# Gate and up of 15 of 22 FFN chunks by seven block products for eight, with the token sums held where x and f were

## The chip, the cores and the metric

The kernel runs on one core of a Trainium2 chip. The metric is the device time of one execution in microseconds (us). The engines are TensorE (PE, matmuls; PEld its weight loads), VectorE (DVE), ScalarE (ACT), GpSimd (POOL) and SyncE (SP, which issues most of the DMAs). Each works through its own queue in order; semaphores tie them together.

## The reference

Two layers of a backbone with 640 tokens (128 context, 512 latent) and 1024 features. Each layer is a half-step FFN, a token mixer and a second half-step FFN, each between norms with gains, shifts and gates that come from a conditioning vector (the modulation). The part that matters here is the FFN:

```python
D_MODEL, D_FF, DEPTH = 1024, 2816, 2        # 128 context and 512 latent tokens

def swiglu(h, w_gu, w_dn):
    g, u = jnp.split(h @ w_gu, 2, axis=-1)
    return (jax.nn.silu(g) * u) @ w_dn

    # in a layer, three times with other weights (the middle one is the mixer):
    mods = (silu(cond) @ w_mod[l] + b_mod[l]).reshape(Bc, 9, 1, D_MODEL)
    f = swiglu(pre(x, 0), w_ffn_gu[l, 0], w_ffn_dn[l, 0])
    x = x + 0.5 * mods[:, 2] * rmsnorm(f, g_post[l, 0])
```

## The kernel before, in words

Features lie on the partitions, tokens along the free axis. Every fp32 operand is kept as a pair (h, lo) with h + lo the value, and every product is three matmuls: h h, lo h, h lo. A matmul takes 128x128 weights and 320 tokens, half of the 640. The input of an FFN is `self.h`, two tiles [128, 8, 640]; the residual x and the branch f are two more tiles of that size, and the four share the slots A to D.

D_FF is 22 chunks of 128. A gate or an up of a chunk (`gate`, `up`) is 8 feature chunks x 3 x 2 halves = 48 matmuls. ScalarE takes the tanh of the gate, DVE makes gate times sigmoid (L535) and the product with up (L540), and the result is split again (L165 ScalarE, L166 DVE) into `act`. `PARTS` cuts the chunks in 7, 7, 8; after each of the first two parts eight `down` tasks (one for 128 features of the output) multiply `act` with the down weights and put or add the result into f on DVE.

The middle of an FFN works on both halves of the tokens. Its two ends are by halves: `boundary` runs the tail of one stage (for an FFN: two chunks and the eight last downs) for one half of the tokens and then the other, and the norm chains (`chain`) of the finished half beside the other half's products; the first five chunks of the next FFN (`NHEAD`) follow in the same way. `STEPS` says how many steps of a chain go ahead of each task.

What comes when on an engine is the order in which `run` emits the tasks. Each weight unit (128 x 1024 for gate and up) is loaded by SP into a ring of three `raw` tiles and split by `split` (ScalarE: wh, DVE: wl, rings of three); `advance` emits the splits two units ahead of the task that uses them. `self.later` holds the splits of activations back until those are out. `self.side` is a generator of modulation steps for later layers (`mods`): one step loads 512 KB of w_mod (two `wm` buffers) and runs two 1024-wide reductions on DVE (L294). Tasks of the middle emit one each (`side`), and whatever is left is emitted by `end` when the FFN is over. The first FFN has 48 such steps to do, the second 48, the third 32, the fourth none.

PSUM tiles are [128, 2, 512], four of them. GpSimd (L334, L340, L446, L917) and the DMAs on its queue work for the norm chains and the mixers.

## Time and profile before

| what | value |
|---|---|
| median of 3 runs | 3243.14 us (3242.57 to 3244.58) |
| span of the profiled execution | 3243.3 us, 50877 instructions |
| PE busy | 3117.2 us, 20988 matmuls |
| DVE busy | 2005.3 us |
| ACT busy | 1162.5 us |
| POOL busy | 496.5 us |
| DMA | 381.51 MB, mean 118 GB/s |

Busy times are of one engine; they overlap. The span is from the first to the last instruction of the execution that was profiled, and the single runs above were made without the profiler. A stretch (a window of the span) gives the busy time of each engine in it, the granted clock of TensorE as a share of full speed (PEclk; full is 2.4 GHz) and the mean busy share of the 16 DMA engines. Line numbers are those of the kernel before; helpers such as `split` and `projs` carry the lines of very many instructions.

### The profile page before, as it was taken

What the parts mean: (1) busy time and instruction counts of PE and PEld (TensorE: products, weight loads), DVE (VectorE), ACT (ScalarE), POOL (GpSimd) and SP (SyncE); (2) the same over time, 40 slices, a digit from 0 to 9 for tenths busy, and PEclk for the clock granted to TensorE, in tenths of its full rate; (3) what the DMA queues carried; (4) which work ended last, traced back from release to release, by engine and by line L of the source; (5) the groups of instructions that cost most, each with busy time, mean ns of one, the idle gap of its engine ahead of it and who ended that gap; (6) DMA issues with size and microseconds to landing.
All of it is one profiled execution on the core that took longest, in us unless ns stands there. A gap on an engine that the chain in (4) does not pass through costs nothing.

```text
span 3243.3 us, 50877 instructions
## 1 busy us (share of the span) xinstructions
PE 3117.2 (96%) x20988; PEld 3081.5 (95%) x20988; DVE 2005.3 (62%) x2880; ACT 1162.5 (36%) x1919; POOL 496.5 (15%) x413
## 2 busy tenths in 40 slices
PE   7999998899999989999989999989999999899997
PEld 6999998899999979999989999989999998899997
DVE  7667649876653485676785663678665436723346
ACT  4222235454432452212452212463444325422123
POOL 4000015500011330000230000244000113200004
PEclk9999999999999999999999999999999999999999
DMA  5454433311122334454434442442111323322223
GB/s 190 170 171 153 145 112 133 128 64 63 58 97 86 133 130 157 149 174 151 137 128 158 150 148 74 134 159 75 66 52 64 103 94 132 129 80 69 82 92 117
DMA packets 118718, 381.51 MB, mean 118 GB/s; under 512 B 13651, under 2 KB 30867, under 8 KB 117461
## 3 DMA queue, kind: packets, MB, share of 16 engines
q1 hardware_dynamic: 115348, 359.73, 33.3%
q0 software_dynamic: 2848, 18.35, 1.5%
q8 instruction: 165, 2.70, 0.3%
q14 instruction: 69, 0.56, 0.1%
q10 hardware_dynamic: 288, 0.17, 0.0%
HBM read 363.88 MB, written 14.32 MB: 117 GB/s over the span
## 4 chain that ended last, share of the span: by engine, by line
PE 80%; DVE 13%; issue 3%; ACT 3%; POOL 0%; DMA 0%; SPq 0%; DVEq 0%; ACTq 0%; POOLq 0%
PE ps L230 74%; DVE wl L166 3%; PE ps L211 2%; PE ps L213 2%; PE ps L212 2%; DVE slotD L366 1%; ACT wh L165 1%; DVE W L1039 1%; DVE slotB L366 1%; DVE t L402 1%; PE ps L257 1%; PE ps L1030 1%; DVE junk L1285 1%; DVE s L340 1%; DVE t L246 0%
## 5 line engine op out<-in xcount | busy, mean ns | idle before, releaser
L166 DVE TENSOR_TENSOR wl<-raw,wh 128x1024 fp32r<-128x1024 f32 (+1 forms) x493 | 616.1, 1251 | 258.3 <-ACT wh L165 247.8
L165 ACT CAST wh<-raw 128x1024 fp32r<-128x1024 f32 (+1 forms) x493 | 507.4, 1032 | 661.9 <-issue 407.2
L230 PE MATMUL ps<-slotA,wh 128*128 128x320 f32 x2272 | 584.6, 313 | 6.1 <-ACT wh L165 3.8
L230 PE MATMUL ps<-slotA,wl 128*128 128x320 f32 x2272 | 580.6, 312 | 6.3 <-DVE wl L166 6.2
L230 PE MATMUL ps<-slotD,wh 128*128 128x320 f32 x2272 | 570.0, 313 | 17.0 <-DVE slotD L1317 15.0
L230 PE MATMUL ps<-slotB,wh 128*128 128x320 f32 x2272 | 580.2, 311 | 3.1 <-DVE slotB L423 1.6
L230 PE MATMUL ps<-act,wh 128*128 128x320 f32 x2816 | 568.5, 310 | 7.6 <-DVE act L166 4.0
L230 PE MATMUL ps<-slotC,wh 128*128 128x320 f32 x2272 | 570.5, 313 | 3.8 <-ACT slotC L413 1.9
L230 PEld LDWEIGHTS ps<-act,wh 128*128 128x128 f32 x2816 | 455.3, 189 | 10.1 <-DVE act L166 5.2
L230 PEld LDWEIGHTS ps<-slotD,wh 128*128 128x128 f32 x2272 | 396.8, 190 | 19.9 <-DVE slotD L1317 16.2
L230 PEld LDWEIGHTS ps<-slotA,wl 128*128 128x128 f32 x2272 | 399.0, 190 | 10.3 <-DVE wl L166 9.2
L230 PEld LDWEIGHTS ps<-slotA,wh 128*128 128x128 f32 x2272 | 398.6, 190 | 9.3 <-ACT wh L165 4.8
L230 PEld LDWEIGHTS ps<-slotB,wh 128*128 128x128 f32 x2272 | 398.5, 190 | 4.5 <-DVE slotB L423 2.2
L230 PEld LDWEIGHTS ps<-slotC,wh 128*128 128x128 f32 x2272 | 396.7, 191 | 5.4 <-ACT slotC L413 2.1
L446 POOL TENSOR_TENSOR s<-s,t 128x320 f32<-128x320 f32 x84 | 118.3, 1408 | 1693.4 <-ACT t L445 1693.2
L230 PE MATMUL ps<-act,wl 128*128 128x320 f32 x1408 | 363.1, 309 | 0.0
L230 PE MATMUL ps<-slotC,wl 128*128 128x320 f32 x1440 | 348.3, 312 | 1.3 <-DVE wl L166 1.1
L294 DVE CUSTOM_DVE_ANT_0 junk<-wm,sc,par 128x1024 bf16<-128x1024 f32 x256 | 328.2, 1282 | 4.8
L230 PEld LDWEIGHTS ps<-slotC,wl 128*128 128x128 f32 x1440 | 248.5, 191 | 2.5 <-DVE wl L166 2.2
L230 PEld LDWEIGHTS ps<-act,wl 128*128 128x128 f32 x1408 | 247.1, 189 | 0.2
L535 DVE SCALAR_TENSOR_TENSOR t<-t,ps 128x640 f32<-128x640 f32 (+1 forms) x111 | 75.6, 681 | 255.3 <-ACT t L534 255.3
L230 PE MATMUL ps<-slotD,wl 128*128 128x320 f32 x832 | 220.7, 312 | 2.1 <-DVE wl L166 2.1
(283 smaller groups left out, 3684.8 us busy)
## 6 DMA issues: line engine op xcount, KB each, us to landing
raw<-in_w_gu SPq DMA_DIRECT2D x222, 512.0 KB, 3.3
wm<-in_w_mod SPq DMA_DIRECT2D x144, 512.0 KB, 3.3
raw<-in_w_dn SPq DMA_DIRECT2D x64, 512.0 KB, 3.5
raw<-in_w_gate SPq DMA_DIRECT2D x64, 512.0 KB, 3.4
raw<-in_w_dn SPq DMA_DIRECT2D x64, 448.0 KB, 4.0
raw<-in_w_in SPq DMA_DIRECT2D x44, 512.0 KB, 3.3
raw<-in_w_o SPq DMA_DIRECT2D x32, 512.0 KB, 3.3
sraw<-in_w_br SPq DMA_DIRECT2D x80, 128.0 KB, 2.0
```

Source lines behind the costliest of these rows:

```text
L165: self.nc.scalar.copy(h, src)
L166: self.nc.vector.tensor_sub(lo, src, h.bitcast(F32))
L211: nc.tensor.matmul(out, sh, mh, start=(k == 0), stop=False)
L212: nc.tensor.matmul(out, sh, ml, start=False, stop=False)
L213: nc.tensor.matmul(out, sl, mh, start=False, stop=(k == n - 1))
L230: nc.tensor.matmul(ps[:, hf, :HW], st[:, ws], m[:, k0 + k, hf * HW:(hf + 1) * HW], start=(first and k == 0 and i == 0), stop=(last and k = ...
L257: nc.tensor.matmul(ps[:, i, :HW], self.ones, ssq[:, i * HW:(i + 1) * HW], start=True, stop=True)
L294: nc.vector.tensor_tensor_reduce(junk, wm, self.sc[:, j, :], 0.5, self.par[l][:, C_BMOD + ch:C_BMOD + ch + 1], ALU.mult, ALU.add, self.mod ...
L340: (nc.vector if ahead or c % 4 == 0 else nc.gpsimd).tensor_add(acc, acc, q)
L366: nc.vector.scalar_tensor_tensor(x, t, gain, x, op0=ALU.mult, op1=ALU.add)
L446: nc.gpsimd.tensor_add(ssq[:, s], ssq[:, s], q)
L535: nc.vector.scalar_tensor_tensor(v, v, 1.0, p, op0=ALU.add, op1=ALU.mult)
```

## The change

The gate and the up of a chunk, for two halves of the tokens and two halves of the features, are eight block products. In 15 chunks of each FFN (all that lie behind the first part and ahead of the tail) they are made of seven, as by Strassen. For that GpSimd makes four sums of weights per chunk (`make_piece`, each 128x512), from which come four pieces (b, 2, u, g) of 1024, 512, 1024 and 1024 columns that are split where there were two of 1024. The token side needs four sums of quarters of `self.h`; these are made once per FFN by `sums`, one step beside each of the eight downs of the first part, and lie in the slots of x and f. So x waits in DRAM (`spill`, or the input in the first FFN), and f too: every down reads and writes `d_f`, and `tail_begin` fetches both back. `PARTS` becomes 5, 5, 6, 6. A block emits one modulation step where gate and up emitted two; a gate or up of the first FFN's first part emits two.

```diff
-PARTS = (7, 7, 8)   # how the chunks of D_FF are cut
+PARTS = (5, 5, 6, 6)
+HK = KC // 2 * P
+def pieces(gate, up):
+    env = {}
+    return tuple(Piece(k, gate, up, env) for k in ("b", "2", "u", "g"))
...
+            if isinstance(ap, Piece):
+                if ap.kind == "b":
+                    e = ap.env
+                    e["g"] = self.unit_tile(False, 2 * HK, F32, "raw")
+                    e["u"] = self.fp.tile([P, 2 * HK], F32, tag="ru", name=self.nm("ru"), bufs=2)
+                    self.nc.sync.dma_start(e["g"], ap.gate)
+                    self.nc.sync.dma_start(e["u"], ap.up)
...
+    def make_piece(self, p):
...
+        add = nc.gpsimd.tensor_add
+        if p.kind == "2":
+            h, lo = (self.fp.tile([P, HK], F32R, tag=t, name=self.nm(t)) for t in ("wh2", "wl2"))
+            self.split(h, lo, e["t2"])
+            return h, lo
+        h = self.unit_tile(False, 2 * HK, F32R, "wh")
+        lo = self.unit_tile(False, 2 * HK, F32R, "wl")
+        self.split(h, lo, u if p.kind == "u" else g)
+        if p.kind == "b":
+            t2 = e["t2"] = self.fp.tile([P, HK], F32, tag="wt", name=self.nm("wt"))
+            add(g[:, one], g[:, one], u[:, one])
+            add(t2, g[:, one], u[:, two])
+            add(u[:, one], u[:, one], u[:, two])
+            add(g[:, two], g[:, two], t2)
+        return h, lo
...
+        def spill():
+            nc.gpsimd.dma_start(self.d_x, self.x)
+            self.gens["sums"] = sums()
+        def tail_begin():
+            self.f = self.slot(self.fs, F32)
+            self.x = self.slot(self.xs, F32)
...
+            for c in range(KC):
+                nc.gpsimd.dma_start(self.f[:, c, fst], self.d_f[c][:, fst])
+            src = a["x"] if first else self.d_x
+            nc.gpsimd.dma_start(self.x[:, :, fst], src[:, :, fst])
...
+        def sums():
...
+            for k in range(KC // 2):
+                a1, a2, s31, s24 = (self.t6() for _ in range(4))
+                for d, c in ((a1, k), (a2, KC // 2 + k)):
+                    nc.gpsimd.tensor_add(d, f(self.h[0][:, c, :]), f(self.h[1][:, c, :]))
+                dve.tensor_sub(s31[:, two], a1[:, two], a2[:, two])
+                dve.tensor_sub(s31[:, one], a1[:, one], a1[:, two])
+                dve.tensor_sub(s24[:, one], s31[:, two], a1[:, one])
+                dve.tensor_add(s24[:, two], a2[:, one], s24[:, one])
+                yield
+                v = lambda t: t.rearrange("p (a b) -> p a b", a=2)
+                for i, t in ((2, s24), (0, s31)):
+                    self.split(sa[:, i:i + 2, k, :], sb[:, i:i + 2, k, :], v(t))
+                yield
+        def block(j, jj):
+            def fn(wb, w2, wu, wg2):
...
+                product(X, quarter(0, 0), wb, 0, True)
+                nc.scalar.copy(k1, X)
+                self.flush()
+                product(Z, quarter(0, 1), wb, 1, True)
+                nc.vector.tensor_add(t[:, one], k1, Z)
+                ahead(1)
+                if self.side is not None:
+                    next(self.side, None)
+                product(X, S2, w2, 0, False)
+                nc.scalar.copy(k2, X)
+                e1, e2 = self.t3(), self.t3()
+                nc.scalar.activation(e1, t[:, one], AF.Tanh, scale=0.5)
+                nc.vector.scalar_tensor_tensor(t[:, one], e1, 1.0, t[:, one], op0=ALU.add, op1=ALU.mult)
+                product(Y, S1, wg2, 0, True)
+                nc.scalar.copy(k5, Y)
+                product(X, S3, wu, 0, False)
+                nc.vector.tensor_sub(u[:, two], k5, X)
+                ahead(2)
+                product(Y, S4, wu, 1, False)
+                nc.vector.tensor_sub(u[:, one], Y, k2)
+                nc.vector.tensor_mul(t[:, one], t[:, one], u[:, one])
+                ahead(3)
+                product(X, quarter(1, 1), wg2, 1, False)
+                nc.scalar.activation(e2, X, AF.Tanh, scale=0.5)
+                nc.vector.scalar_tensor_tensor(t[:, two], e2, 1.0, X, op0=ALU.add, op1=ALU.mult)
+                nc.vector.tensor_mul(t[:, two], t[:, two], u[:, two])
...
+                ahead(4)
...
+                elif part:
+                    mid.append(block(j, jj))
...
-                    fv = self.f[:, c, :].rearrange("p (a b) -> p a b", a=2)
                     if part == 0:
-                        nc.scalar.copy(fv, ps[:, :, :HW])
+                        nc.scalar.copy(tv, ps[:, :, :HW])
                     else:
-                        nc.vector.tensor_add(fv, fv, ps[:, :, :HW])
+                        nc.vector.tensor_add(tv, tv, ps[:, :, :HW])
+                        load_f(c + 2)
+                    nc.gpsimd.dma_start(self.d_f[c], t)
...
-        for i in (10, 20, 30):
-            mid[i].side += 1
+        for t in mid:
+            if t.name in ("gate", "up"):
+                t.side += 1
```

`product` is twelve matmuls (four feature chunks x three), `ahead(n)` emits the splits of the next block's first n pieces, X, Z and Y are banks of PSUM.

On DVE, one chunk in the middle of the second FFN was this before (wl a weight split, junk the two reductions of a modulation step, L535 and L540 the readouts of gate and up):

```order
L166 TENSOR_TENSOR wl_14476<-raw_14345,wh_14475 128x1024
L166 TENSOR_TENSOR act_13840<-t_1854_14402,act_13839 128x640
L535 SCALAR_TENSOR_TENSOR t_1869_14530<-t_1869_14530,ps_14481 128x640
L294 ISA junk_14535,mod_92<-wm_14467,sc_10979,par_90 128x1024
L294 ISA mod_92 128x1
L294 ISA junk_14537,mod_92<-wm_14467,sc_10979,par_90 128x1024
L294 ISA mod_92 128x1
L166 TENSOR_TENSOR wl_14542<-raw_14411,wh_14541 128x1024
L540 TENSOR_TENSOR t_1869_14530<-t_1869_14530,ps_14545 128x640
```

After the change a block there goes like this, from the first activation half to the next block's first weight split (its modulation step follows):

```order
L655 SCALAR_TENSOR_TENSOR t_2709_17682<-t_2720_17743,t_2709_17682 128x320
L659 TENSOR_TENSOR t_2710_17683<-t_2713_17686,ps_17680 128x320
L219 TENSOR_TENSOR wl_2723_17774<-wt_17717,wh_2722_17773 128x512
L662 TENSOR_TENSOR t_2710_17683<-ps_17681,t_2712_17685 128x320
L663 TENSOR_TENSOR t_2709_17682<-t_2709_17682,t_2710_17683 128x320
L219 TENSOR_TENSOR wl_17796<-ru_17667,wh_17795 128x1024
L667 SCALAR_TENSOR_TENSOR t_2709_17682<-t_2721_17744,ps_17680 128x320
L668 TENSOR_TENSOR t_2709_17682<-t_2709_17682,t_2710_17683 128x320
L219 TENSOR_TENSOR wl_17815<-raw_17666,wh_17814 128x1024
L219 TENSOR_TENSOR act_17679<-t_2709_17682,act_17678 128x640
L647 TENSOR_TENSOR t_2732_17820<-t_2734_17822,ps_17819 128x320
L219 TENSOR_TENSOR wl_17854<-raw_17791,wh_17853 128x1024
```

Two long readouts have become seven short operations, and four weight splits stand among them where there were two.

On POOL nothing stood between the norm chains of an FFN's head and the squares of its tail. Now, at the end of the second FFN's first downs, there are the token sums (L608), the stores of f (L788) and the first blocks' sums of weights (L210 to L213):

```order
L788 DMA d_f<-s_2656_17444 128x640
L608 TENSOR_TENSOR t_2664_17461<-slotA_16225,slotB_16226 128x640
L608 TENSOR_TENSOR t_2665_17462<-slotA_16225,slotB_16226 128x640
L788 DMA d_f<-s_2669_17502 128x640
L788 DMA d_f<-s_2676_17550 128x640
L210 TENSOR_TENSOR raw_17453<-raw_17453,ru_17454 128x512
L211 TENSOR_TENSOR wt_17563<-raw_17453,ru_17454 128x512
L212 TENSOR_TENSOR ru_17454<-ru_17454 128x512
L213 TENSOR_TENSOR raw_17453<-raw_17453,wt_17563 128x512
L608 TENSOR_TENSOR t_2683_17568<-slotA_16225,slotB_16226 128x640
L608 TENSOR_TENSOR t_2684_17569<-slotA_16225,slotB_16226 128x640
L788 DMA d_f<-s_2688_17609 128x640
```

Each pair of token sums has a store of f ahead of it, and the last pair four sums of weights as well.

On DVE at the switch from the second FFN (of layer 0) to the third, this stood before, the last input of the finished half, then a split, the other half's Newton steps (L244 to L248) and the new FFN's first readout:

```order
L423 TENSOR_TENSOR slotB_15366<-t_2010_15454,slotA_15365 128x320
L435 TENSOR_TENSOR slotC_12020<-slotC_12020,ps_15505 128x320
L419 SCALAR_TENSOR_TENSOR slotB_15366<-t_2017_15501,mod_92,slotA_15365 128x320
L166 TENSOR_TENSOR wl_15544<-raw_15445,wh_15543 128x1024
L244 SCALAR_TENSOR_TENSOR t_2031_15578<-t_2031_15578,t_2030_15577 128x320
L245 SCALAR_TENSOR_TENSOR s_1881_14605<-t_2031_15578,s_1881_14605 128x320
L246 SCALAR_TENSOR_TENSOR t_2031_15578<-s_1881_14605,t_2030_15577 128x320
L247 TENSOR_TENSOR t_2031_15578<-t_2031_15578,s_1881_14605 128x320
```

Now the rows between that last input (L473) and the split are 20 reductions, of which these are the last three, and the Newton steps (L298 and on) stand behind them:

```order
L348 ISA junk_16423,mod_92<-wm_16413,sc_11427,par_90 128x1024
L348 ISA mod_92 128x1
L348 ISA junk_16425,mod_92<-wm_16419,sc_11427,par_90 128x1024
L348 ISA mod_92 128x1
L348 ISA junk_16427,mod_92<-wm_16419,sc_11427,par_90 128x1024
L348 ISA mod_92 128x1
L362 SCALAR_TENSOR_TENSOR co_93<-mod_92,par_90 128x8 x2
L219 TENSOR_TENSOR wl_16440<-raw_16293,wh_16439 128x1024
L298 SCALAR_TENSOR_TENSOR t_2515_16474<-t_2515_16474,t_2514_16473 128x320
L299 SCALAR_TENSOR_TENSOR s_2339_15543<-t_2515_16474,s_2339_15543 128x320
```

They are the modulation steps of the second FFN for which its tasks have no place any more.

## Rows read from the trace of the kernel before

**Rows 1.** The page: busy us (share of the span) and instructions of each engine

```profile
PE 3117.2 (96%) x20988; PEld 3081.5 (95%) x20988; DVE 2005.3 (62%) x2880; ACT 1162.5 (36%) x1919; POOL 496.5 (15%) x413
```

**Rows 2.** The page: the chain that ended last, by engine

```profile
PE 80%; DVE 13%; issue 3%; ACT 3%; POOL 0%; DMA 0%; SPq 0%; DVEq 0%; ACTq 0%; POOLq 0%
```

**Rows 3.** The chain in order of time: start us, us, what

```profile
1199.71 390.40 PE ps L230 x2660
...
1617.31 3.54 PE ps L230 x24
```

**Rows 4.** Stretches: the second FFN's middle, first, third and last boundary

```profile
core 0: us, PE busy (x) PEld busy (x) DVE busy (x) ACT busy (x) POOL busy (x), PEclk, DMA share, GB/s
1200.00:1560.00 360.00, 360.00 (x2456) 360.00 (x2456) 244.14 (x343) 92.66 (x118) 0.00 (x0) 1.00 0.48 156
490.00:540.00 50.00, 44.59 (x292) 42.73 (x291) 45.99 (x64) 28.73 (x50) 23.69 (x19) 1.00 0.40 131
1596.00:1640.00 44.00, 39.67 (x247) 38.23 (x246) 40.85 (x54) 24.37 (x43) 22.52 (x18) 0.94 0.43 141
1640.00:1686.00 46.00, 38.01 (x234) 36.23 (x233) 40.29 (x63) 23.07 (x43) 21.73 (x19) 0.94 0.30 107
3150.00:3243.00 93.00, 74.65 (x501) 73.19 (x499) 56.80 (x79) 30.52 (x46) 34.13 (x28) 0.93 0.38 122
```

**Rows 5.** DVE in order of time, second FFN's middle: start us, us, instruction

```profile
1502.14 0.82 DVE L540 TENSOR_TENSOR t<-t,ps 128x640 f32<-128x640 f32 x1 [1.81 <-PE ps L230]
1502.88 1.28 DVE L294 CUSTOM_DVE_ANT_0 junk<-wm,sc,par 128x1024 bf16<-128x1024 f32 x1
...
1505.41 1.22 DVE L166 TENSOR_TENSOR wl<-raw,wh 128x1024 fp32r<-128x1024 f32 x1
1506.55 0.82 DVE L166 TENSOR_TENSOR act<-t,act 128x640 fp32r<-128x640 f32 x1
```

**Rows 6.** DVE in order of time, where the third FFN begins

```profile
1639.23 0.47 DVE L435 TENSOR_TENSOR slotC<-slotC,ps 128x320 f32<-128x320 f32 x1
1639.63 0.54 DVE L419 SCALAR_TENSOR_TENSOR slotB<-t,mod,slotA 128x320 fp32r<-128x320 f32 x1
1641.18 1.23 DVE L166 TENSOR_TENSOR wl<-raw,wh 128x1024 fp32r<-128x1024 f32 x1 [1.01 <-ACT wh L165]
1643.88 0.49 DVE L244 SCALAR_TENSOR_TENSOR t<-t,t 128x320 f32<-128x320 f32 x1 [1.47 <-ACT t L241]
```

**Rows 7.** POOL in order of time, three places

```profile
500.39 0.86 POOL L334 TENSOR_TENSOR t<-slotB,s 128x320 f32<-128x320 f32 x1 [1.29 <-DVE s L340]
...
681.10 1.62 POOL L917 TENSOR_TENSOR s<-t,t 128x640 f32<-128x640 f32 x1 [27.93 <-DVE t L911]
...
1013.68 2.44 POOL L921 TENSOR_TENSOR s<-s,t 128x640 f32<-128x640 f32 x1 [16.92 <-DVE t L911]
```

**Rows 8.** DVE at the second and third of these places

```profile
682.30 0.83 DVE L777 TENSOR_TENSOR t<-ps,sa 32x640 f32<-32x640 f32 x1 [1.01 <-ACT t L944]
...
1013.46 1.22 DVE L166 TENSOR_TENSOR wl<-raw,wh 128x1024 fp32r<-128x1024 f32 x1
```

**Rows 9.** POOL and DVE in order of time, first boundary

```profile
491.31 7.80 POOL L334 TENSOR_TENSOR t<-slotB,s 128x320 f32<-128x320 f32 x6 [5.71 <-DVE s L248]
...
493.19 1.17 DVE L166 TENSOR_TENSOR act<-t,act 128x320 fp32r<-128x320 f32 x1
494.29 2.26 DVE L366 SCALAR_TENSOR_TENSOR slotA<-t,co,slotA 128x320 f32<-128x320 f32 x2
```

**Rows 10.** DMA issues: count, KB each, median us from issue to landing

```profile
wm<-in_w_mod SPq DMA_DIRECT2D x144, 512.0 KB, 3.3
...
d_acc<-s POOLq DMA_DIRECT2D x16, 320.0 KB, 2.6
s<-d_acc SPq DMA_DIRECT2D x16, 320.0 KB, 2.8
```

**Rows 11.** The page: GB/s in 40 equal slices of the span

```profile
GB/s 190 170 171 153 145 112 133 128 64 63 58 97 86 133 130 157 149 174 151 137 128 158 150 148 74 134 159 75 66 52 64 103 94 132 129 80 69 82 92 117
```

More of the change, by code (lines that the diff above doesn't have):

```diff
@@ L58, with __init__ @@
 class Task:
-    def __init__(self, name, fn, units=(), side=0, gen=(None, 0), ahead=2):
+    def __init__(self, name, fn, units=(), side=0, gen=(None, 0), ahead=2, flush=True):
         self.name, self.fn, self.units, self.side, self.gen, self.ahead = name, fn, units, side, gen, ahead
+        self.flush = flush
+class Piece:
+    def __init__(self, kind, gate, up, env):
+        self.kind, self.gate, self.up, self.env = kind, gate, up, env
+def pieces(gate, up):
+    env = {}
+    return tuple(Piece(k, gate, up, env) for k in ("b", "2", "u", "g"))
 class Kernel:
@@ L142, in advance @@
             r = st["raw"].pop(0)
+            if isinstance(r, Piece):
+                st["out"].append(self.make_piece(r))
+                st["split"] += 1
+                continue
             w = r.shape[-1]
@@ L161, in fetch @@
             st["dma"] += 1
+    def make_piece(self, p):
+        nc = self.nc
+        e = p.env
+        g, u = e["g"], e["u"]
+        one, two = slice(0, HK), slice(HK, 2 * HK)
+        add = nc.gpsimd.tensor_add
[13 more added lines that the diff above has]
+        return h, lo
     def split(self, h, lo, src):
@@ L179, in run @@
         self.later = []
-        small = lambda u: u.shape[-1] <= 256
+        small = lambda u: not isinstance(u, Piece) and u.shape[-1] <= 256
         self.streams = [dict(plan=[u for t in tasks for u in t.units if small(u) == k],
@@ new lines, in sums @@
+        def sums():
+            sa, sb = (self.slots.tile([P, 4, KC // 2, HW], F32R, tag=t, name=self.nm("s")) for t in (self.xs, self.fs))
+            S["S"] = [(sa[:, i], sb[:, i]) for i in range(4)]
+            one, two = slice(0, HW), slice(HW, T)
+            f = lambda t: t.bitcast(F32)
+            dve = nc.vector
+            for k in range(KC // 2):
[11 more added lines that the diff above has]
+                yield
@@ new lines, in block, with product @@
+        def block(j, jj):
+            def fn(wb, w2, wu, wg2):
+                if jj == 0:
+                    new_act(j)
+                got = self.streams[False]["get"]
+                more = isinstance(self.streams[False]["plan"][got], Piece)
+                ahead = lambda n: self.advance(False, got + (n if more else max(1, n - 1)))
+                xx, zy = self.ps(), self.ps()
+                X, Z, Y = xx[:, 0, :HW], zy[:, 0, :HW], zy[:, 1, :HW]
+                S3, S1, S2, S4 = S["S"]
+                quarter = lambda r, k: [x[:, k * KC // 2:(k + 1) * KC // 2, r * HW:(r + 1) * HW] for x in self.h]
+                def product(o, a, w, part, new):
+                    n = KC // 2
+                    for k in range(n):
+                        ws = slice(part * HK + k * P, part * HK + (k + 1) * P)
+                        for i, (x, y) in enumerate(((0, 0), (1, 0), (0, 1))):
+                            nc.tensor.matmul(o, w[x][:, ws], a[y][:, k, :], start=(new and k == 0 and i == 0),
+                                             stop=(k == n - 1 and i == 2), skip_group_check=not new)
+                t, u = self.t6(), self.t6()
+                one, two = slice(0, HW), slice(HW, T)
+                k1, k2, k5 = self.t3(), self.t3(), self.t3()
+                product(X, quarter(0, 0), wb, 0, True)
+                nc.scalar.copy(k1, X)
+                self.flush()
+                product(Z, quarter(0, 1), wb, 1, True)
[21 more added lines that the diff above has]
+                nc.vector.tensor_mul(t[:, two], t[:, two], u[:, two])
+                h, lo = (x[:, jj, :] for x in S["act"])
+                self.later.append(lambda: self.split(h, lo, t))
+                if not more:
+                    self.flush()
+                ahead(4)
+            return Task("block", fn, pieces(wg[j, 0], wg[j, 1]), ahead=0, flush=False)
@@ L590, in first_fn @@
                 begin()
+                self.gens["sums"] = sums()
                 new_act(0)
@@ L630, in dn2 @@
             return Task("down2", fn, (wd[c][:, j0 * P:NJ * P],))
-        for i in (10, 20, 30):
-            mid[i].side += 1
+        for t in mid:
+            if t.name in ("gate", "up"):
+                t.side += 1
         tail += [lambda hf, c=c: dn2(c, hf) for c in range(KC)]
-        return head, pair, mid, tail, begin, end
+        return head, pair, mid, tail, begin, end, spill, tail_begin
     def views(self, t, ps, halves):
```

33 lines of the change are left out of this document (27 added, 6 removed).

## The prediction

> **What bounds the kernel now.** I read the page's table of engines first, then the chain that ended last, the stretches, and in the stretches the vector engine (DVE) and GpSimd (POOL) in order of time. The table shows TensorE (PE) busy 96%, DVE 62%, POOL 15% [rows 1]; the chain gives PE 80% and DVE 13% [rows 2]. So PE sets the time, except in the boundaries: one piece of the chain is 390.40 us of 2660 matmuls without a break [rows 3], which is 0.1468 us a matmul, while around the norms PE idles 4 to 8 us in each stretch of some 45 us and DVE is busy 40 of them [rows 4]. In the middle of an FFN POOL does nothing (0.00 of 360 us) and DVE is busy 68% [rows 4]. The span, 3243.3 us, is 0.16 us above the median of the three runs; nothing lies around it, so I sum against 3243.3.
>
> **What goes.** A chunk's gate and up are 96 matmuls (14.10 us); by seven products they are 84 (12.33 us). 60 chunks (15 in each of four FFNs) lose 720 matmuls: **-105.7 us** at 0.1468, if PE alone decides. Down and its last part only move: 7, 7, 8 chunks become 5, 5, 6, 6, the sum of matmuls stays.
>
> **What comes, 1: the blocks.** Per block I count what DVE does, by the spacing of its instructions [rows 5]: three splits of 1024 at 1.14 (3.42), one of 512 (0.58, between 1.14 and the 0.40 of a 320-wide one [rows 6]), the activation's split 0.74, seven 320-wide operations at 0.40 (2.80), and one modulation step, 2.53 for its two halves. That is 10.07 us, or 7.54 where no step is left. Against 12.33 us of PE it would fit. But POOL now makes four sums of 128x512 per block. Alone, POOL's 128x320 takes 0.86 and its 128x640 1.62 [rows 7], so 512 is about 1.3. And POOL and DVE do not overlap: a 640-wide sum that meets a split that had begun takes 2.44, though the split keeps its 1.22 [rows 7, 8]; where POOL has six operations queued, DVE's 320-wide operations take 1.13 to 1.17 instead of 0.48 and POOL's six take 7.80 instead of 5.2 [rows 9]. They go by turns, an instruction each. Only a DVE operation with one operand in PSUM runs on beside it: 0.83 beside the 1.62 of 681.10 [rows 7, 8].
>
> The Trainium skill, "SBUF — State Buffer", section "Who interferes with whom", says that a VectorE instruction with two SBUF inputs and a GpSimd instruction that reads SBUF block each other wholly, and that order of issue decides who waits. The rows agree. By that rule the sum is the one below, 3278; were the port's bandwidth split instead, each would be slowed a little, blocks would stay near 12.4 us, and the time would be that of the first rival, 3184.
>
> In rows 9 a DVE operation loses 0.73 us (1.13 less 0.40) to a POOL operation of 0.86. A sum of 1.3 then costs 1.1, four of them 4.4; DVE has four operations with a PSUM operand per block in which a part is lost to nobody, so I take 4.0 (from 0, all hidden, to 5.2, all waited for). A block with a modulation step is then 10.07 + 4.0 = 14.1 us, as long as the 14.10 it replaces: +1.77 against PE's 12.33. Without a step it is 11.5, and PE's 12.33 holds. ScalarE gets a few short readouts and casts more; it is busy 92.66 of 360 us in such a stretch [rows 4], so they cost nothing by themselves. PE waits for DVE in a block because the fifth product must be read out of PSUM before the seventh adds to the same bank, and because the splits of the next block stand in the same queue.
>
> Steps are left for 11 blocks of the first FFN (49 steps: 14 in the first gates and ups, 8 downs, 5 blocks, 8 downs, 6 blocks, 8 downs), for all 15 of the second (48 to do, 39 places) and 11 of the third (33). 37 x 1.77 = 65.5. DVE catches up in the downs: with five chunks a down is 4.40 us of PE against 0.74 + 0.74 + 2.53 = 4.01 of DVE, 3.1 us over eight, in three FFNs 9.3; with six chunks 1.1 each, which covers the last four blocks of the second FFN, 7.1. **+49** (0 to 109, at 15.3 a block).
>
> **2: the token sums**, beside the first eight downs of each FFN. Per two downs (8.81 us of PE) DVE has two splits (1.48), four subtractions (1.60), two splits of the sums (1.48) and two steps (5.06): 9.62, and POOL two 640-wide sums, 3.2, which stand behind the store of the down before, so that DVE's subtractions, and all behind them, wait. Together 12.8 if nothing overlaps: +4.0 per two, +16 per FFN; with all hidden +3.2, which two units of lead take up. POOL's place behind the stores puts it near the upper end: 14 in each of three FFNs. In the last one, without steps, 4.56 + 3.2 fits, but its last two sums stand behind four sums of the first block's weights (5.2), and the third product waits for their split: 5. **+47** (0 to 56).
>
> **3: the modulation that is left over.** In the second FFN 10 of 48 steps have no place and are issued in one go when the FFN ends, ahead of the next FFN's norms, readouts and splits on DVE. DVE: 25.3 us; with two buffers, 3.3 us from issue to landing [rows 10] and 2.53 of use, two steps need 5.8, so ten take 5.1 + 4 x 5.8 = 28.4. In the trace of before DVE is free for 1.01 us there and then has a split and the Newton steps of the other half [rows 6], and 5.7 of the 46 us that follow are idle on it [rows 4]. PE has the pair (7.05 us) to do and then nothing: **+26** (16, if pair and idle cover their part, to 28).
>
> **4: shorter tails.** The last part has 6 chunks in place of 8, so a half's eight last downs take 21.1 us instead of 28.2, and the norms of the other half beside them lose 7.05 us of cover. In the first boundary DVE is busy 45.99 of 50 us, in the third 40.85 of 44 [rows 4]: it is the bound, and saves 8 x (1.14 - 0.87) = 2.2. So 4.9 stays as idle PE in three of four; in the last DVE is busy 57 of 93 and I take nothing. **+15** (0 to 28).
>
> **5: x and f from DRAM.** A store takes 2.6 us to land, a load 2.8 [rows 10]; loads run two downs ahead. The stretch of 156 GB/s has the DMA engines busy 0.48 [rows 4], which makes some 325 at full use; eight downs with load, store, weights and a modulation load want 1.51 MB in 4.40 us, 343 GB/s. The shortfall is 0.24 us a down, 24 downs, half of it hidden: **+3** (0 to 6). x and f for the tail are wanted 14 us and more after they are asked for; that cover is the four gates and ups of the first half.
>
> **Sum.** 3243.3 - 105.7 + 49 + 47 + 26 + 15 + 3 = 3277.6: **3278 us**, 1.1% slower. With every cost at its lower end 3154, at its upper 3365.
>
> **Rivals.**
> *The sums hide.* Place: the blocks; mechanism: POOL's sums fall into DVE's operations with a PSUM operand and into its waits for ScalarE. For it: DVE's own 10.07 is below 12.33, and four such operations of 0.40 are there. Against: rows 9, and that a block has 1.6 us of them for 5.2 us of sums. Then blocks cost 0, the first downs 11, the left-over steps 22, tails 10, DRAM 3: 3243.3 - 105.7 + 46 = 3184. It decides from about 13.2 us a block with a step: below that the sum is under 3243. Half of the gain in the fourth FFN, which has no steps, is mine too.
> *POOL is the chain.* The four sums are in series behind a split, and each may run at the ratio of 2.44 to 1.62: 2.0 us, 8.0 a block, all in DVE's way. Blocks with a step 17, without 15.5: 37 x 4.7 + 23 x 3.2 = 248 in place of 49, 3477. Against: a DVE that waits leaves POOL the next turn at once.
> *DMA.* If the loads of the downs get no more than the best slice of the page, 190 GB/s [rows 11], a down of the second group takes 7.95 us (+3.5), one of the third 8.3 (+3.0): 24 x 3.5 + 22 x 3.0 = 150 more, 3428. Against: 156 GB/s needs only half the engines' time.
> *The products don't cost what I think.* A stationary block now serves one moving half. Weights are already loaded once per matmul (20988 of each [rows 1]), and tasks by halves run at the same 0.147 a matmul, 24 in 3.54 us [rows 3]; I give this nothing.
>
> **Chances.** Forecast's mechanism 0.64, sums hidden 0.25, POOL's chain 0.05, DMA 0.06. Range for 8 in 10: 3185 to 3345; it cuts off half of the first rival's lower side and both of the slow ones. A measurement of this kernel tells 0.2% (6.5 us) from no change. Faster by more: 0.25 (the first rival, and the forecast's own best corner, less that rival's worst). Within: 0.07. Slower: 0.68.
>
> **What would show it.** In the profile after: 720 matmuls fewer than the 20988 of [rows 1], PE's own time down by some 106 us; in a block of the second FFN products five to seven spread over 14 us, PE waiting for DVE's readout of the fifth; 320-wide DVE operations of over 1 us there, and POOL's 512-wide sums of 1.3 alone and above 2 behind a split; a block of the last FFN at 12.3 us. At the end of the second FFN a stretch of about 20 us with DVE at modulation only and PE idle, its granted clock under 1 there, as the 0.94 of the stretches with idle PE [rows 4]. First downs with steps at about 6 us each in place of 4.40, PE waiting for splits. The forecast is wrong if blocks with steps run below 13.2 us (the turns are then not the price), or if blocks without steps stay above 12.5 (POOL's chain), or if PE waits in the downs for DMA.

## The result, and the profile after

The changed kernel takes 3336.49 us (median of four runs, 3335.39 to 3342.41), beside 3243.41 us (3242.57 to 3244.58) for the kernel before on the same chip: ratio 1.0295, interval 1.0281 to 1.031. Slower was forecast, and the time lies in the range, but the change is +93 us where +35 was forecast. Line numbers from here on are those of the changed kernel.

The table of engines of the profile after, beside [rows 1]:

```profile
span 3333.6 us, 51825 instructions
PE 3068.8 (92%) x20268; PEld 3010.1 (90%) x20268; DVE 2433.5 (73%) x3460; ACT 1367.7 (41%) x2343; POOL 1029.1 (31%) x856
```

The 720 matmuls are gone as forecast, yet PE's busy time fell by 48 us, not 106, and its share fell from 96% to 92%. DVE has 428 us more and POOL 533. Of the 58 us between 48 and 106 some 36 are TensorE's clock: by the spacing of their starts, 680 matmuls ran at 0.22 to 0.30 us each where 361 did before (an estimate from the two traces).

The stretches of the second FFN, which answer to the first row of [rows 4] (columns: stretch, its length, busy us of each engine, granted clock of TensorE, DMA share, GB/s). In order: all up to the first block's end, with a part of the first downs at the seam to the first block (a seam is the change from downs to blocks) and the 17 us behind it; the rest of the first five blocks; the second downs with the first block behind them; the rest of the second group; the third downs with a block; the last group.

```profile
1221.00:1337.00 116.00, 100.84 (x644) 98.83 (x643) 86.42 (x126) 46.40 (x73) 33.48 (x29) 0.91 0.53 182
1274.00:1320.00 46.00, 34.20 (x228) 33.14 (x226) 35.59 (x51) 16.52 (x25) 19.19 (x18) 0.92 0.43 150
1320.00:1337.00 17.00, 14.49 (x72) 13.82 (x73) 16.89 (x22) 5.34 (x9) 7.17 (x4) 0.71 0.68 255
1337.00:1390.00 53.00, 50.43 (x339) 49.40 (x338) 50.25 (x65) 23.69 (x39) 22.85 (x12) 1.00 0.26 87
1390.00:1449.00 59.00, 51.73 (x332) 50.54 (x331) 49.99 (x65) 14.74 (x21) 19.23 (x16) 0.94 0.75 262
1449.00:1517.00 68.00, 63.27 (x414) 61.88 (x413) 64.17 (x82) 29.86 (x47) 30.02 (x16) 0.97 0.28 94
1517.00:1578.00 61.00, 57.39 (x374) 56.72 (x373) 50.91 (x67) 14.96 (x20) 19.30 (x16) 0.94 0.73 258
1578.00:1617.00 39.00, 37.34 (x252) 36.66 (x251) 36.88 (x48) 17.97 (x29) 17.60 (x13) 1.00 0.30 102
```

No stretch has PE at its full length any more. In the blocks DVE is busy 95% (50.25 of 53), so it is the bound there; in the later downs it is at 85% and the DMA engines at 0.75, so something else is waited for as well.

What PE waited for (us in total, times, longest):

```profile
PE ps L637 <- ACT t L644: 57.8, 10, 10.6
PE ps L284 <- DVE wl L219: 37.8, 22, 24.7
PE ps L637 <- DVE t L659: 26.0, 27, 2.2
```

Three causes can be told apart. 24.7 of the second row is the burst of left-over modulation at the second FFN's end. The third row is the fifth product's readout in 27 blocks, some 1 us each. The first is new: the third product of the first block of a group, which waits for a ScalarE copy (L644) that stands behind much else. It is 10.6 us in the first group of the first three FFNs, 5.3 to 5.6 in their second, and 5.1 in the first group of the last FFN.

A block of the second group, DVE, ACT and POOL in order of time:

```profile
1448.69 0.49 DVE L668 TENSOR_TENSOR t<-t,t 128x320 f32<-128x320 f32 x1
...
1452.50 1.28 DVE L348 CUSTOM_DVE_ANT_0 junk<-wm,sc,par 128x1024 bf16<-128x1024 f32 x1
1452.66 2.27 POOL L210 TENSOR_TENSOR raw<-raw,ru 128x512 f32<-128x512 f32 x1 [5.89 <-DVE wl L219]
...
1453.82 2.19 DVE L348 CUSTOM_DVE_ANT_0 junk<-wm,sc,par 128x1024 bf16<-128x1024 f32 x1
...
1455.02 2.16 POOL L211 TENSOR_TENSOR wt<-raw,ru 128x512 f32<-128x512 f32 x1
...
1455.95 1.57 DVE L655 SCALAR_TENSOR_TENSOR t<-t,t 128x320 f32<-128x320 f32 x1
1457.45 0.47 DVE L659 TENSOR_TENSOR t<-t,ps 128x320 f32<-128x320 f32 x1
...
1457.97 0.42 PE L637 MATMUL ps<-slotA,wh 128*128 128x320 f32 x1 [0.92 <-DVE t L659]
...
1462.29 0.49 DVE L668 TENSOR_TENSOR t<-t,t 128x320 f32<-128x320 f32 x1
```

These are the turns that were forecast: POOL's 1.28 us sum takes 2.27, DVE's 1.28 reduction 2.19, its 320-wide operation 1.57 in place of the 0.47 that L659 takes. From one L668 to the next is 13.6 us (1462.29 less 1448.69; forecast 14.1), while a block of the fourth FFN, without steps, takes 12.3. Most blocks with a step take 13.6; some late in a group take 14.2 to 15.4, for which no cause was sought, and the last of a group 11.2. So far the forecast holds. It fails at the seams. POOL, and under it DVE, ScalarE and PE, where the second FFN's first downs end:

```profile
1305.89 1.28 POOL L210 TENSOR_TENSOR raw<-raw,ru 128x512 f32<-128x512 f32 x1 [5.68 <-DVE wl L219]
1307.24 1.30 POOL L211 TENSOR_TENSOR wt<-raw,ru 128x512 f32<-128x512 f32 x1
1308.50 1.29 POOL L212 TENSOR_TENSOR ru<-ru 128x512 f32<-128x512 f32 x1
1309.74 1.26 POOL L213 TENSOR_TENSOR raw<-raw,wt 128x512 f32<-128x512 f32 x1
1310.96 3.02 POOL L608 TENSOR_TENSOR t<-slotA,slotB 128x640 f32<-128x640 f32 x2
```

```profile
1303.37 1.28 DVE L348 CUSTOM_DVE_ANT_0 junk<-wm,sc,par 128x1024 bf16<-128x1024 f32 x1
1304.58 0.08 DVE L348 DVE_READ_ACCUMULATOR2_ANT mod<- 128x1 f32 x1
1304.58 1.22 DVE L219 TENSOR_TENSOR wl<-raw,wh 128x1024 fp32r<-128x1024 f32 x1
1314.01 0.49 DVE L609 TENSOR_TENSOR t<-t,t 128x320 f32<-128x320 f32 x1 [8.21 <-POOL t L608]
```

```profile
1315.87 1.35 ACT L218 CAST s<-t 128x640 fp32r<-128x640 f32 x2 [6.68 <-DVE t L612]
...
1319.60 0.42 ACT L644 COPY t<-ps 128x320 f32<-128x320 f32 x1
...
1320.08 0.63 PE L637 MATMUL ps<-s,wh 128*128 128x320 f32 x1 [10.59 <-ACT t L644]
```

The first block's split comes late behind modulation steps, the four weight sums follow in series, the last token sums stand behind them, and DVE then waits 8.21 us. ScalarE's casts of the token sums wait for DVE, and the copy that PE needs stands behind them. A queue in which everything is in order turned a backlog on DVE into idle time on DVE. PE stands still for 10.6 us there, and is slower when it resumes:

```profile
1310.00:1320.00 10.00, 0.00 (x0) 0.00 (x0) 5.92 (x11) 4.13 (x6) 5.02 (x5) 0.63 0.16 55
1320.00:1330.00 10.00, 7.87 (x29) 7.47 (x30) 9.93 (x12) 2.30 (x5) 3.05 (x2) 0.51 0.87 325
```

The second row has 29 matmuls in 7.87 us, 0.27 us each, at a granted clock of 0.51: the lower of the two levels, 1.2 GHz. That this lengthened anything is not shown: DVE is busy 9.93 of these 10 us, and PE waits for it again in them (2.05 us at 1325.70). And in the second downs, SP's queue:

```profile
1401.09 0.33 SPq L732 DMA_DIRECT2D s<-d_f  x1
1401.51 0.38 SPq L336 DMA_DIRECT2D wm<-in_w_mod  x1
1401.98 0.39 SPq L190 DMA_DIRECT2D raw<-in_w_dn  x1
1408.68 0.33 SPq L732 DMA_DIRECT2D s<-d_f  x1
1409.11 1.10 SPq L336 DMA_DIRECT2D wm<-in_w_mod  x1
1410.30 0.38 SPq L184 DMA_DIRECT2D raw<-in_w_gu  x1
```

Between 1402.4 and 1408.7 it issues nothing: the next load of f goes into a buffer whose store has to land first, and the loads of w_mod and of weights stand behind it. In the whole run SP waits 169.7 us in 38 such places, and DVE waits 34.6 us in 25 places for a load of w_mod, most of them in the later downs; in the kernel before DVE has no such wait.

```profile
SPq L732 <- DMA d_f<-s: 169.7, 38, 8.0
DVE junk L348 <- DMA wm<-in_w_mod: 34.6, 25, 3.6
```

Landings became longer too, beside [rows 10]:

```profile
wm<-in_w_mod SPq DMA_DIRECT2D x144, 512.0 KB, 3.8
...
d_f<-s POOLq DMA_DIRECT2D x96, 320.0 KB, 4.0
```

### The profile page after: what moved, and what is told of

The parts are those of the page before. It is cut to its first block, busy times and chain, and to the rows that moved or that the text cites. A ratio compares the mean times of both kernels' runs of the same rounds, so it can differ in the third digit from the quotient of the medians.

```text
span 3333.6 us, 51825 instructions
## 1 busy us (share of the span) xinstructions
PE 3068.8 (92%) x20268; PEld 3010.1 (90%) x20268; DVE 2433.5 (73%) x3460; ACT 1367.7 (41%) x2343; POOL 1029.1 (31%) x856
## 5 line engine op out<-in xcount | busy, mean ns | idle before, releaser
L219 DVE TENSOR_TENSOR wl<-raw,wh 128x1024 fp32r<-128x1024 f32 (+3 forms) x525 | 623.5, 1189 | 183.0 <-ACT wh L218 175.0
L218 ACT CAST wh<-raw 128x1024 fp32r<-128x1024 f32 (+3 forms) x525 | 506.7, 967 | 460.8 <-PE ps L284 231.5
L637 PE MATMUL ps<-s,wh 128*128 128x320 f32 x1920 | 456.2, 322 | 66.6 <-ACT t L644 57.8
L637 PEld LDWEIGHTS ps<-s,wh 128*128 128x128 f32 x1920 | 341.0, 197 | 74.2 <-ACT t L644 60.5
L348 DVE CUSTOM_DVE_ANT_0 junk<-wm,sc,par 128x1024 bf16<-128x1024 f32 x256 | 366.1, 1430 | 39.7 <-DMA wm<-in_w_mod 34.6
L284 PE MATMUL ps<-slotA,wl 128*128 128x320 f32 x1312 | 364.9, 316 | 31.5 <-DVE wl L219 31.2
L284 PE MATMUL ps<-slotA,wh 128*128 128x320 f32 x1312 | 368.2, 318 | 9.3 <-ACT wh L218 6.6
L284 PE MATMUL ps<-slotB,wh 128*128 128x320 f32 x1312 | 363.6, 315 | 2.2 <-DVE slotB L477 1.1
L284 PE MATMUL ps<-slotD,wh 128*128 128x320 f32 x1312 | 351.2, 316 | 14.8 <-DVE slotD L1485 12.7
L284 PE MATMUL ps<-slotC,wh 128*128 128x320 f32 x1312 | 351.3, 316 | 7.5 <-ACT wh L218 3.1
L637 PE MATMUL ps<-s,wl 128*128 128x320 f32 x960 | 306.7, 319 | 0.0
L284 PEld LDWEIGHTS ps<-slotD,wh 128*128 128x128 f32 x1312 | 235.1, 192 | 18.2 <-DVE slotD L1485 14.1
L210 POOL TENSOR_TENSOR raw<-raw,ru 128x512 f32<-128x512 f32 x60 | 106.8, 1779 | 356.8 <-DVE wl L219 356.8
```

The source lines that it names most:

```text
L210: add(g[:, one], g[:, one], u[:, one])
L218: self.nc.scalar.copy(h, src)
L219: self.nc.vector.tensor_sub(lo, src, h.bitcast(F32))
L284: nc.tensor.matmul(ps[:, hf, :HW], st[:, ws], m[:, k0 + k, hf * HW:(hf + 1) * HW], start=(first and k == 0 and i == 0), stop=(last and k = ...
L348: nc.vector.tensor_tensor_reduce(junk, wm, self.sc[:, j, :], 0.5, self.par[l][:, C_BMOD + ch:C_BMOD + ch + 1], ALU.mult, ALU.add, self.mod ...
L637: nc.tensor.matmul(o, w[x][:, ws], a[y][:, k, :], start=(new and k == 0 and i == 0), stop=(k == n - 1 and i == 2), skip_group_check=not new)
```

## The experiments

Where nothing else is said, a version was timed once, beside the kernel before on the same chip (3240.7 to 3243.7 us). The four times of the changed kernel lie 7 us apart, so a difference of a few us between single times means nothing. The fences show the edits cut to the lines that matter; "..." stands for what is left out.

**No modulation steps**, in the changed kernel and in the kernel before (all coefficients but the first FFN's are left out).

```diff
-        todo = {(0, 0): sec(0, range(2, 8)), (0, 2): ..., (1, 0): sec(1, range(5, 9)), (1, 2): []}
+        todo = {(0, 0): [], (0, 2): [], (1, 0): [], (1, 2): []}
```

> The changed kernel without the modulation steps beside the FFNs (left out: the modulation of all but the first FFN's input; constants stand in its place). Theory A, the modulation steps make the loss (in the blocks by turns with GpSimd, at the seams where a late step holds back the first weight piece, and in the 20 left over): every FFN middle then costs what the last one costs now, 8 us over the pure gain in place of 55, 52, 41, and the 25 us hole goes: 3336 - 47 - 43 - 32 - 26 = about 3188. Theory B, the weight and token sums on GpSimd hold TensorE up by themselves, steps or not: the seams stay (16 us in each of three FFNs) and so does some of the blocks: about 3250.

> The kernel before without the modulation steps (the same part left out), as the baseline of x1. Both theories: TensorE was without a gap in the middles, so nothing to gain there; 0 to 8 us at the boundaries: 3235 to 3243.

3190.75 us and 3238.22 us, as theory A had it. The steps cost the kernel before 5 us and the changed one 146. Without them seven products win 47 us. PE's busy time is 3027.7 us there, 41 less than with them for the same matmuls.

```profile
1176.00:1279.60 103.60, 97.18 (x641) 96.43 (x641) 66.90 (x92) 46.13 (x73) 32.10 (x29) 0.96 0.46 153
1279.60:1328.80 49.20, 49.20 (x338) 49.20 (x337) 37.05 (x47) 23.58 (x39) 16.99 (x12) 1.00 0.19 60
1328.80:1376.60 47.80, 47.80 (x328) 47.80 (x328) 24.83 (x31) 14.44 (x20) 15.50 (x16) 1.00 0.63 215
```

These are the stretches of its second FFN (to the first block's end, four blocks, second downs with a block). Blocks and downs are pure PE; only the first stretch is not, as in the fourth FFN of the changed kernel. I use this run as the base of a table of us in order. Every FFN is cut at the end of the last Newton step of the norm ahead (L298) and at the last DVE operation of blocks (L668); "downs" are the second or third downs with the first block behind them.

| FFN, kernel | to the first block's end | four blocks | second downs | five blocks | third downs | three blocks |
|---|---|---|---|---|---|---|
| 1, changed | 187.3 | 54.5 | 58.5 | 65.6 | 60.6 | 36.9 |
| 1, without steps | 167.9 | 49.2 | 47.7 | 61.4 | 54.8 | 36.7 |
| 2, changed | 116.2 | 52.3 | 59.2 | 68.1 | 61.4 | 39.0 |
| 2, without steps | 103.6 | 49.2 | 47.7 | 61.4 | 54.8 | 36.8 |
| 3, changed | 116.9 | 52.3 | 57.7 | 68.1 | 55.4 | 36.9 |
| 3, without steps | 105.0 | 49.2 | 47.7 | 61.4 | 54.8 | 36.8 |
| 4, changed | 103.5 | 49.2 | 47.7 | 61.4 | 54.8 | 36.7 |
| 4, without steps | 103.6 | 49.2 | 47.7 | 61.4 | 54.8 | 36.7 |

Summed over the FFNs the steps cost 43.8 ahead of the first block's end, 31.6 in the blocks and 45.3 in the later downs with their seams; the boundary behind the second FFN (first to last of its Newton steps) takes 104.7 in place of 77.1, 27.6 more.

**Weight sums: left out, and moved to DVE.** In the first, the four sums of weights are left out.

```diff
             t2 = e["t2"] = self.fp.tile([P, HK], F32, ...)
-            add(g[:, one], g[:, one], u[:, one])
...
-            add(g[:, two], g[:, two], t2)
```

```diff
-        add = nc.gpsimd.tensor_add
+        add = nc.vector.tensor_add
```

> The changed kernel with the steps but without GpSimd's four sums of weights (left out; the pieces are split from the raw gate and up). If the sums are half of the loss (turns with DVE in blocks, and a chain of four at each seam): blocks with a step 12.4 in place of 13.6 (37 of them, 40 us) and the seams 5 to 8 us less in three FFNs, three each (50 us): about 3245. If only the turns in the blocks: about 3295. If neither, because loads and steps are late by themselves: above 3315.

> Changed kernel, the four weight sums of a block on VectorE instead of GpSimd. Leaving them out altogether gave 3265. If their price is the serial chain on GpSimd and its turns with VectorE, 60 times four sums of 0.58 us on VectorE cost part of 139 us that lies beside TensorE: 3280 to 3310. Rival, VectorE's busy time is what counts in the blocks and all of the 139 us ends on the path: 3380 to 3404.

3264.82 us, 72 less, between two of the expected values: blocks with steps fall to 12.3 us, and the rest comes from the seams (the second stretch of the table 49.3, the third 55.7 in the second FFN). With the sums on DVE 3336.26, no change, which neither theory had. Blocks with steps take 14.0 us instead of 13.6, and PE's stalls of 10.6 us at the first blocks give way to pairs of 3.6 and 3.3 to 4.4 us. So four sums on POOL lengthened a block about as much as four sums that DVE made itself (13.6 and 14.0 us, against 12.3 without sums). In four such blocks DVE is busy 48.49 of 54.30 us, here without any POOL:

```profile
1336.60:1390.90 54.30, 50.10 (x338) 49.32 (x337) 48.49 (x76) 23.48 (x39) 0.00 (x0) 1.00 0.25 84
```

**f's trip: left out, and its loads on another queue.** In the first, f's parts are not stored (but for the last) and the load is a fill with zeros on POOL (0.63 us each), so parts of f are left out.

```diff
-                nc.sync.dma_start(t, self.d_f[c])
+                nc.gpsimd.memset(t, 0.0)
```

```diff
-                nc.sync.dma_start(t, self.d_f[c])
+                nc.gpsimd.dma_start(t, self.d_f[c])
...
-                        load_f(c + 2)
                     nc.gpsimd.dma_start(self.d_f[c], t)
+                    if part:
+                        load_f(c + 2)
```

> The changed kernel without f's way through DRAM between the parts (left out: the sum of f over the parts; GpSimd clears the tile instead, only the third group's result is stored). Theory DMA, the downs of the second and third group have the DMA queues full, so that DVE waits for the modulation's loads and the first block's weight is late: those seams fall from 12 and 7 us to 3 each in three FFNs: about 3300. Theory A or B without DMA: less than 10 us, above 3325.

> Changed kernel (3336), but f's loads in the later downs are issued by GpSimd, each behind the store of its down, instead of by SP. In the trace of the changed kernel SP's queue waits up to 8 us at such a load for an earlier store out of the same buffer (169.7 us in 38 waits), and the loads of w_mod and of weights stand behind it. If that queue is the price of f's trip (27 us by the run without the trip): 3309 to 3321. Rival, the trip costs by its traffic (the transfers' share of the DMA engines): within 6 us of 3336.

3309.32 us: the trip costs 27, not 3. In the last FFN, which has no steps, it costs nothing (the six stretches are the same to 0.1 us with and without it). With the loads on POOL's queue 3322.82, just above the range expected: half of it, 14 us, was the blocked SP queue, and DVE's waits for w_mod fall from 34.6 us to 5.9 (4.8 without the trip). Second downs with a block go from 59.2 to 56.2 us in the second FFN (53.7 without the trip). So the other half is not a wait for these loads; whether traffic or the round trip itself holds it was not separated.

**Token sums: earlier, left out, and without steps beside them.** The second takes the quarters themselves for their sums; the third leaves out the steps of the first gates, ups and downs.

```diff
-... gen=("sums", int(part == 0))))
+... gen=("sums", 2 * int(part == 0))))
```

```diff
-                S3, S1, S2, S4 = S["S"]
+                S3, S1, S2, S4 = quarter(0, 0), quarter(0, 1), quarter(1, 0), quarter(1, 1)
```

```diff
-... Task("down", dn, (...), 1, gen=...)
+... Task("down", dn, (...), int(part > 0), gen=...)
             if t.name in ("gate", "up"):
-                t.side += 1
+                t.side = 0
...
+        todo = {k: v[:max(0, len(v) - (22 if k == (0, 0) else 8))] for k, v in todo.items()}
```

> Changed kernel (3336), but the token sums take two steps per first down, so that they are through by the fourth down instead of the last and no longer stand on GpSimd behind the first block's weight sums. If the first seam's stall of 10.6 us is made by that queue, three seams lose some 5 to 8 us each: 3312 to 3322. Rival, VectorE's total between the seams sets the time and work that is moved only waits elsewhere: within 5 us of 3336.

> Changed kernel without the sums of quarters of the normed tokens (left out: the products take the quarters themselves). If the token sums are the price of the stretch before the first block (44 us with steps and some 9 us an FFN without them): 3336 - 60 to 80 = 3256 to 3276. Rival, the price is the steps and the seam with the first block's weight sums, and the token sums mostly hide: 3311 or more.

> Changed kernel without the modulation steps of the first gates, ups and downs (these coefficients are left out; those in blocks and later downs stay, and the ten left over at the end of the second FFN too). If the stretch is lost because VectorE has the steps and the token sums there together, it falls to what it is without any steps: 3336 - 35 to 44 = 3292 to 3301. Rival, the token sums' own chain through GpSimd, VectorE and ScalarE is the price, whatever stands beside it: 3320 or more.

3339.22, 3281.33 and 3285.95 us. Early sums leave 3.7 us of the 10.6 us stall (second FFN), and gain nothing: PE waits 3.8 us for a weight split in the first downs instead, so the work only waits elsewhere, as the rival had it. Leaving out the sums gains 55, leaving out the steps 50, where neither expectation allowed for both. The two prices do not add: the second FFN's first stretch is 103.6 us with sums only, 100.9 with steps only, 116.2 with both, and some 96.2 with neither (an estimate: 103.6 less the 7.4 that the sums cost in the fourth FFN, 103.5 less 96.1). Alone 7.4 and 4.7, together 20.0.

**The steps of the later downs left out, and the steps dealt anew.** The first leaves out 16 steps of each of the first three FFNs, so that the ten that are left over stay.

```diff
-... Task("down", dn, (...), 1, gen=...)
+... Task("down", dn, (...), int(part == 0), gen=...)
...
+        todo = {k: v[:max(0, len(v) - 16)] for k, v in todo.items()}
```

```diff
+        rest = sec(0, range(2, 9)) + sec(1, range(9))
-        todo = {(0, 0): sec(0, range(2, 8)), ...}
+        todo = {(0, 0): rest[:52], (0, 2): rest[52:90], (1, 0): rest[90:120], (1, 2): rest[120:]}
```

> Changed kernel without the modulation steps of the second and third downs (16 steps fewer in each of the first three FFNs; these coefficients are left out). Between the groups of blocks the changed kernel loses 45 us against the run without any steps. If the steps there take VectorE's last slack: 3291 to 3301. Rival, the forecast's view that VectorE has slack in those downs and catches up for the blocks: the loss stays in the blocks or grows there, 3320 or more.

> Changed kernel with the 128 modulation steps dealt anew over the four FFNs (52, 38, 30, 8), so that none is left over at the end of the second FFN. If the leftover burst is worth its 24.7 us gap and the moved steps cost in the fourth FFN what they cost elsewhere (about 1 us each, from 146 us less 25 for 118 steps): about 3311. If they cost nothing there: 3303. Rival, the burst covers other work that comes late without it: 3330 or more.

3293.48 us, 43 less, as the first theory had it. The later downs and their seams lose 37.6: 49.7 in place of 59.2 in the second FFN, 54.8 in place of 60.6 in the first. Most blocks stay at 13.6 us; those that took 14.2 to 15.4 are fewer, which gives another 7 us. So these downs had no slack to give to the blocks; they were over-full themselves. Dealt anew: 3324.19. The burst is gone (its boundary takes 77.3 us), but the eight steps that went to the fourth FFN stand beside its token sums, and its first stretch takes 116.1 us instead of 103.5: half of the gain is given back, more than the expected 1 us a step.

**Versions that use it.** First, seven products in the last FFN only; then in the last two, with all 128 steps beside the first two FFNs (64 each); then this with the weight sums on DVE and five buffers in place of three for f's trip, which have room there because these FFNs hold no modulation. `ffn_old` is the FFN of eight products of the kernel before. Five runs each.

```diff
-   ... = self.ffn(l, st, todo[l, st], prev is None)
+   ... = (self.ffn if (l, st) == (DEPTH - 1, 2) else self.ffn_old)(l, st, todo[l, st], prev is None)
```

```diff
+   ... = (self.ffn if l else self.ffn_old)(l, st, todo[l, st], prev is None)
+        todo = {(0, 0): rest[:64], (0, 2): rest[64:], (1, 0): [], (1, 2): []}
```

```diff
+        add = nc.vector.tensor_add
+        sf = lambda: self.fp.tile([P, T], F32, tag="sf", name=self.nm("sf"), bufs=5)
```

> Eight products in the first three FFNs, as before; seven products, token sums and the trip through DRAM only in the last FFN, which has no modulation steps. If the loss comes with the steps, the last FFN keeps what it gained in the changed kernel (10.9 us in its middle, 7.0 us in its end): 3243 - 18 = 3225, range 3217 to 3232. Rival, that gain hung on what the three FFNs before it had left: 3240 to 3250.

> Eight products in the first two FFNs, with all 128 modulation steps beside them (64 each, some gates and ups take two); seven products in the last two FFNs, without steps. In the run of the changed kernel without steps an FFN's middle is 9 to 11 us shorter than before and the boundary behind it 3 to 7; with 22 more steps in the first two FFNs at little cost: 3216, range 3208 to 3226. Rival, VectorE is full in the first two FFNs with 64 steps each: 3232 or more.

> The kernel with seven products in the last two FFNs and the steps in the first two; the weight sums on VectorE, which has room there without steps, and five buffers instead of three for f's trip. In the run with the sums on VectorE the last FFN's middle was 2.3 us shorter than in the changed kernel: 2 x 2.3 off the kernel with the sums on GpSimd, and 0 to 5 for the buffers: 3204 to 3214. Rival, neither was waited for without steps: within 2 us of the other.

3230.06 us, ratio to the kernel before 0.9965 (0.9951 to 0.9979); 3226.82, 0.9957 (0.9945 to 0.997); 3218.22, **0.993** (0.9917 to 0.9944). All three beat both kernels; the gain on the kernel before is under 1%, but none of the intervals reaches 1. The first lies in its range (3217 to 3232). The second lies just above its range (3208 to 3226): the middles of its first two FFNs, with 64 steps each, are 4.3 and 3.9 us longer than before and the boundary behind the first 5.3. The third gained 8.6 on it where 4.6 to 9.6 was expected, but lies above its range, which counted from the 3216 that the second missed. Which of its two edits did that was not separated; the first stretches of its two FFNs are 3.9 and 3.8 us shorter than the second's, and the sums on DVE alone had shortened that of the last FFN from 103.5 to 98.4, so the record points to the sums. A stretch of its second FFN, with 64 steps and eight products, beside the first row of [rows 4]:

```profile
1200.00:1560.00 360.00, 356.58 (x2416) 355.62 (x2415) 280.82 (x404) 92.87 (x120) 2.62 (x2) 1.00 0.53 176
```

DVE takes 37 us more there and PE loses 3.4: the eight-product FFN has nearly all the room for the steps that the seven-product one has not.

## Why the prediction was wrong

**The step that failed is "DVE catches up in the downs".** The forecast took 16.4 us off the blocks' price for slack in the second and third downs. With the first blocks behind them (four with a step, which it priced at 7.1) that makes -9.3. They lost 45.3 instead, a difference of 55 in a miss of 58. The working set 4.01 us of DVE against 4.40 of PE and took the 0.39 between them as free. It left out that the seam to the next block (a late split, four sums in series, more splits) draws on the same queue, and that DVE in such a down waits for data that SP's queue holds back. Both show in the same stretches: they are 19.4 us shorter without weight sums, 13.0 with f's loads off SP's queue, 37.6 without the steps of these downs (prices that overlap and do not add).

**f and x through DRAM** (+3) was mis-sized by a factor of nine: 27 us. It was worked out as a shortfall of traffic. Half of what it cost is a queue: a load that waits for a store holds up all of SP's later loads. The working did not ask what stands behind a waiting load on SP. Most of the 27 lies in the later downs, so it is a part of the 45.3 and not to be added to it.

**The token sums** (+47) were too low: leaving them out gains 55 us, and the whole stretch lost more. In the second FFN steps and sums together cost 20.0 where 14, and 1.8 for the first block's step, were taken; that is above the 16 that the working gave for nothing hidden. What it left out is the seam. That the last token sums stand behind the first block's weight sums it counted for the last FFN alone, at 5, and there PE's stall is 5.1 (7.4 by leaving the sums out); in the first three FFNs, where steps stand in the same queue, the stall is 10.6 (5.1 in all four without steps). POOL's place behind the stores, the reason that it gave, was not tested by itself.

**The blocks** were priced too high: 30 of the 37 with a step lie behind the first of their group, 53 us at 1.77, and they cost 31.6: most take 13.6 us instead of 14.1, and the last of each group, which has no sums of a next block beside it, 11.2. The mechanism was right. What the Trainium skill states in "SBUF — State Buffer", section "Who interferes with whom", that a VectorE instruction with two SBUF inputs and a GpSimd instruction that reads SBUF block each other as a whole, agrees with the 2.19 and 1.57 us above, and with the 0.47 of L659, which has one input in PSUM. Blocks without steps keep PE's 12.3, as forecast.

**The left-over burst** (+26) measured 27.6 and is PE's longest wait, 24.7; **the shorter tails** (+15, as 4.9 in three boundaries and nothing in the last) about 15: without steps the boundaries are 0.6, 2.9, 3.2 and 6.8 us shorter than before where 7.05 us of PE left each, so 6.5, 4.2, 3.9 and 0.3 stayed (some 4 us more in all beside the kernel before without steps, whose own boundaries are shorter).

Of the rivals, "the sums hide" is refuted (13.6 us is above its 13.2), "POOL is the chain" holds for the first block of a group only, and "DMA" named the right place for the wrong reason: the downs do wait for loads, but for 14 us by a queue, not for 150 by a rate. The errors did not all have one sign: that the blocks were 21 too high hid about what the stretches ahead of the first blocks were too low (52 taken with the first blocks' steps; by the table some 73, if the sums cost 7.4 in each FFN). That the time fell inside the range is in part luck: had the blocks cost the 53, it would be some 3358.

## What to carry to other kernels

Before trading matmuls for vector work, ask of every stretch what DVE and POOL have there together, and count the seams, where several units' preparation falls due at once, as stretches of their own; slack that was found in one operation's spacing is not slack if the same queue prepares the next stage. Background work that was free (5 us for 128 steps) can become the most expensive thing in the program (146 us) once its cover is gone, and seven products in the two FFNs that were freed of it gained 23 us where in all four they had lost 93. A load that must wait for a store should not stand in the queue that feeds everything else.

## What the runs showed of the hardware

Weight sums of 128x512 took 1.26 to 1.30 us on POOL where DVE was idle and up to 2.27 by turns, and made on DVE instead they left the time as it was (3336.26 against 3336.49). Stalls of 10.6 us on PE were followed by matmuls at the lower clock: 29 in 10 us at a granted 0.51 behind the second of the three, 28 at 0.53 behind the third, 0.27 us each in place of 0.147; behind the first the mean of such 10 us was 0.68. DVE was busy 9.93 us in each, so what the slower matmuls cost is not shown. DVE's 1024-wide reduction, which I had only seen at 1.28, took 2.19 where a POOL sum ran.
